# A hybrid decoder layer on one core: the first product of two tiles at a time in seven products of halves

## The chip, the cores and the metric

The kernel runs on one core of a Trainium2 chip. The core has five engines with queues of their own: PE (TensorE, the matrix products; PEld is its loading of weights), DVE (VectorE), ACT (ScalarE), POOL (GpSimd) and SP (SyncE, which here only issues DMAs). Each engine takes its instructions in the order in which they stand, and waits on semaphores for the others. Operands lie in SBUF, products in the eight banks of PSUM, inputs and scratch tensors in DRAM. The metric is the time of one execution on the device, in microseconds; less is better.

## The reference, cut to what matters

One layer of a decoder for 1024 tokens of 1024 channels, float32. The change lies in the first product, z, and in attention's output.

```python
u = rmsnorm(h, mix_pre_norm)
z = u @ w_in                                  # the first product
z_attn, z_rwkv, z_gate = ...                  # 2304, 1696 and 2048 columns
o_attn = dilated_attention_branch(z_attn)     # three groups (dilation 1, 4, 16), four heads each
o_rwkv = rwkv7_time_mix(z_rwkv, ...)
gate_attn, gate_rwkv = split(sigmoid(z_gate), 2)
merged = gate_attn * (o_attn @ w_attn_up) + gate_rwkv * (o_rwkv @ w_rwkv_up)
h = h + rmsnorm(merged @ w_out, mix_post_norm)
...                                           # a dense MLP and a gated input embedding
```

In attention each group gives, for each head, an output and a softmax maximum m and sum den; the heads' outputs are added over the three groups with weights exp(m - M) x den / (their sum).

## The kernel before, in words

**Tiles of the first product.** z is made transposed, in 48 tiles of 128 columns of `w_in` (`wz`): 2 for the low-rank inputs, 12 for the RWKV part, 18 for attention and 16 of gates. u lies transposed in SBUF as `uT[p][h]`: p is the high or the low part of a number (the high part is the value rounded to float32r, the low part the rest), h the half of the tokens. A tile's weights come as `wr` by DMA, ACT copies the high part to `wh`, POOL subtracts it to `wl`. Every product of the kernel is made of three: high x high, high x low, low x high (`mm3`). So a tile is 2 halves of tokens x 8 slices of channels x 3 = 48 matmuls of 128x512, 24 to a PSUM bank. Three banks (`z0`, `z1`, `s0`) rotate. When a bank is full, ACT copies it out: for attention into q, k or v with the tokens reordered by the dilation (`qk`, `v`), for a gate into `gst`, which SP stores in DRAM (`gscr`).

**Attention.** A unit n (0 to 5) is two heads of one group; the groups come in the order 2, 1, 0. A unit has three tiles (q, k, v). q and k are turned by rope: SP swaps their halves into `sw` by DMA, POOL multiplies `sw` by the sines, DVE multiplies by the cosines and adds. v is turned by PE (`av`) and copied to `vkb`. Then come four steps r of two blocks: scores on PE (`sc`), masked maxima on DVE (the rows named ISA in the order, CUSTOM_DVE in the profile, `SB<-sc,amask`), `nm` on DVE (minus the maximum), exponentials on ACT (`SB<-SB,nm`), transposes on PE (`pt`), copies on DVE (`PB`), values on PE (`po`), and ACT copies the output out. The outputs of six units stay in SBUF (`OTA`, `OTB`). After the last step `combine` makes the weights of the sum for all four heads, turns them on PE (`rw`), spreads them with `sel` over the channels (`cb`), and DVE and POOL multiply and add. `oaT` is the result's high and low part.

**The merge.** Eight bodies `merge(j)` multiply the RWKV output (`orT`, tiles `orw`, loaded from DRAM by `load_or`) and `oaT` by `wup`, in `bk` and `z` banks, with two gates read back from DRAM (`g<-gscr`).

**What sets the order.** The program is written by a small planner, `Order`. Attention and RWKV are chains, generators that are resumed at their due time. The tiles are dense work: a list of bodies with a gate (a condition) and a load; whenever no chain is due, the next matmul of the current dense body is issued, and the next body is picked from the list, the first whose gate holds. A gate tile of `wz` can be taken at any time, so it fills what attention leaves open. PE keeps the planner's order to the end. DVE, ACT, POOL and SP keep it up to attention; after that a second scheduler orders their instructions. Tiles in SBUF have tags (`TM0`, `MP`, `px`, ...): a new tile with a tag waits until the old one has been read.

Of the kernel before, what the change touches and what calls it, by code (L numbers as in the profile page):

```python
# [19 lines left out]
T = 1024  # L20
# [115 lines left out]

class Order:
# [41 lines left out]
    def pick(self):  # L179
        for i, (gate, load, body, late) in enumerate(self.dense):  # L180
            if gate() if gate else i == 0:
                del self.dense[i]
                return body(*load()) if load else body(), late
        return None
# [60 lines left out]
def layer(ctx: ExitStack, tc: tile.TileContext, x, pT, wz, wup, w_out, wff1, w_ff2, w_ple, w_pleg,  # L245
# [22 lines left out]
    bv_scr = [dram.tile([128, T], F32, name=f"bvscr{w}") for w in range(NU)]  # L268
    og_scr = [dram.tile([128, T], F32, name=f"ogscr{w}") for w in range(NU)]
# [201 lines left out]
    def add_z(wi, evac, gate=None):  # L471
        def body(hi, lo):
            for h in range(2):
                ps = zbank()
                yield from zhalf(ps, hi, lo, h)
                evac(h, ps)
        sch.add(body, lambda: wload(wz[wi]), gate)

    def add_gate(j):
        def evac(h, ps):  # L480
            st = rtile([128, 512], "gst", "gst")
            S.activation(st, ps, AF.Copy)
            SY.dma_start(g_scr[j][:, h * 512:(h + 1) * 512], st)
        add_z(32 + j, evac, lambda: True)
# [428 lines left out]
    def attn_ok(n, x):  # L913
# [3 lines left out]
        return (("Q", n - 2) if x < 2 else ("vk", n - 1)) in done  # L917

    def add_attn(n):
# [7 lines left out]
        def permuted(dst, ps, h):  # L927
            S.activation(dst.rearrange("p (r i) -> p i r", r=d)[:, h * (L // 2):(h + 1) * (L // 2), :],
                         ps.rearrange("p (i r) -> p i r", r=d), AF.Copy)

        def turned(z, sw):
            G.tensor_tensor(sw, sw, rope_t[g][:, 1], OP.mult)
            V.tensor_tensor(z, z, rope_t[g][:, 0], OP.mult)
            yield max(G.end - sch.t, 0.0) + 1.0
# [3 lines left out]
        def qk(x):  # L938
            def evac(h, ps):
                if h == 0:  # L940
                    A[n][x] = rtile([128, T], "qk", (("r", "Ep"), ("k", "En"))[x][hp])
                    if g not in rope_t:
                        rope_t[g] = rtile([128, 2, T], "rope", f"AR{gi % 2}")
                        SY.dma_start(rope_t[g], rope[g].rearrange("a p t -> p a t"))
                z = A[n][x]
                permuted(z, ps, h)
                if h == 1:
# [4 lines left out]
            return evac  # L952

        def v_evac(h, ps):
            if h == 0:
                A[n]["vx"] = rtile([128, T], "v", "v" if n else "TM0")
            permuted(A[n]["vx"], ps, h)
            if h == 1:
                A[n][2] = A[n]["vx"]
                A[n]["t"] = sch.dep  # L960
        for x, evac in enumerate((qk(0), qk(1), v_evac)):
            add_z(base + x, evac, lambda x=x: attn_ok(n, x))
# [3 lines left out]
    def attention():  # L966
# [33 lines left out]
        def nat(g):  # L1000
            NAT[g] = yield from natural(g, stat)

# [3 lines left out]
        OTA = rtile([128, 2, 2, T], "OTA", "TM0")  # L1006
        OTB = rtile([128, 2, 2, T], "OTB", "TM1")
        OT = {g: (OTA[:, 0], OTA[:, 1], OTB[:, 0])[i] for i, g in enumerate(GORD)}

# [8 lines left out]
        def scores(r):  # L1018
# [29 lines left out]
            if r % 8 == 7:  # L1048
                sch.spawn(nat(g), 2, 5.0)
# [15 lines left out]
        def values(r, po):  # L1065
            n, g, hp = unit(r)
            d = DILS[g]
            vk, out_ = vkb[:, n % 2], OT[g][:, hp]
# [8 lines left out]
            if r % 2:  # L1077
                b = 2 * (r % 4)
                src = po.rearrange("p a b -> p (a b)")
# [9 lines left out]
            if r % 4 == 3:  # L1089
                done.add(("B", n))  # L1090
                if n < 4:
                    sch.spawn(at_last(n + 2), 2)
                else:
                    load_or(5 - n, G)
# [21 lines left out]
        load_or(2, G)  # L1116
        load_or(3, V)
# [700 lines left out]
```

## Time and profile before

| what | us |
|---|---|
| median of 3 runs | 1790.07 (1789.71 to 1792.19) |
| the profiled execution | 1786.45 |
| its span, first to last instruction | 1784.7 |
| PE busy in it | 1751.1 (98%) |
| attention's first scores to its last step | about 523 to 778 |
| last matmul of attention's sum (`cb`) | 804 |
| gate tiles alone | 804 to 832 |
| merge | 832 to 900 |

How the rows are read: a group's row has the engine, the operation, out<-in by the names of tiles, the shape, the count, then the busy time in us and the mean of one in ns, and behind the second bar the idle time just before these instructions with what ended it. A row of the timeline begins with the start and the duration in us. A row of a table of stretches has the length and then each engine's busy time, the granted clock of PE, the share of the DMA engines and GB/s.

### The profile page before, as it was taken

To read this page: it belongs to the slowest core of one execution; us is meant where nothing else is said; L and a number is where in the kernel's file an instruction comes from. 1 tells how busy PE (TensorE), PEld (TensorE's weight loads), DVE (VectorE), ACT (ScalarE), POOL (GpSimd) and SP (SyncE) were. 2 spreads that over 40 slices of the span, in tenths; PEclk is the share of its full clock that TensorE was granted. 3 is DMA by queue.
4 is the path that set the end of the run, shared out by engine and by line. 5 is a ranking of instruction groups with operands and counts; after the bars stand their busy time and mean duration, and the time that the engine had idled before them with its cause. 6 is when DMAs were issued, how large, how long until landed. Compare 5 with 4: busy or idle time off the path is not lost.

```text
span 1784.7 us, 25836 instructions
## 1 busy us (share of the span) xinstructions
PE 1751.1 (98%) x10192; PEld 1430.9 (80%) x10192; DVE 1052.5 (59%) x1866; ACT 728.2 (41%) x1301; POOL 773.6 (43%) x507
## 2 busy tenths in 40 slices
PE   9999989999999999999999999999999999999898
PEld 8787877878877877778888888888888888887786
DVE  6289777766535233353736565655655677888454
ACT  5824433332334343542524533333333333334353
POOL 1344131231232323332230366666666897986411
PEclk9999999999999999999999999999999999999999
DMA  4621121212242222333534211121111111113221
GB/s 161 210 95 37 48 77 42 90 42 95 84 146 77 66 60 71 100 120 133 200 95 142 83 60 59 50 69 48 48 48 48 53 54 48 48 48 100 93 79 48
DMA packets 51546, 146.13 MB, mean 82 GB/s; under 512 B 6241, under 2 KB 6625, under 8 KB 51426
## 3 DMA queue, kind: packets, MB, share of 16 engines
q1 hardware_dynamic: 51426, 144.49, 24.7%
q8 instruction: 80, 1.31, 0.3%
q14 instruction: 40, 0.33, 0.1%
HBM read 110.52 MB, written 27.26 MB: 77 GB/s over the span
## 4 chain that ended last, share of the span: by engine, by line
PE 89%; DVE 5%; ACT 3%; issue 2%; POOL 1%; DMA 0%; DVEq 0%; ACTq 0%; POOLq 0%
PE z L293 19%; PE z L295 19%; PE z L291 19%; PE bk L291 7%; PE bk L295 7%; PE bk L293 7%; DVE tot L116 1%; PE sc L274 1%; PE tp L282 1%; DVE xy L116 1%; PE A L274 1%; PE y L274 1%; PE po L274 1%; PE pt L282 1%; PE wr L274 1%
## 5 line engine op out<-in xcount | busy, mean ns | idle before, releaser
L116 DVE TENSOR_TENSOR tot<-tot,bk 128x512 f32<-128x512 f32 x468 | 308.1, 684 | 188.1 <-PE bk L295 187.4
L116 POOL TENSOR_TENSOR wl<-wr,wh 128x1024 fp32r<-128x1024 f32 (+1 forms) x87 | 211.5, 2431 | 442.2 <-ACT wh L116 423.0
L291 PE MATMUL z<-uh,wh 128*128 128x512 f32 (+1 forms) x800 | 313.6, 392 | 5.8 <-ACT part L116 3.0
L295 PE MATMUL z<-uh,wl 128*128 128x512 f32 (+1 forms) x800 | 314.2, 393 | 2.6 <-POOL wl L116 2.6
L293 PE MATMUL z<-ul,wh 128*128 128x512 f32 (+1 forms) x800 | 315.0, 394 | 0.3 <-DVE ul L116 0.3
L293 PE MATMUL z<-f,wh 128*128 128x512 f32 x496 | 193.1, 389 | 0.2 <-DVE f L116 0.2
L291 PE MATMUL z<-f,wh 128*128 128x512 f32 x496 | 193.2, 389 | 0.1
L295 PE MATMUL z<-f,wl 128*128 128x512 f32 x496 | 193.0, 389 | 0.0
L291 PEld LDWEIGHTS z<-uh,wh 128*128 128x128 f32 x800 | 152.0, 190 | 36.9 <-ACT part L116 3.5
L116 ACT ACTIVATE duo<-sum 128x512 fp32r<-128x512 f32 x150 | 90.3, 625 | 222.2 <-PE bk L295 117.1
L295 PEld LDWEIGHTS z<-uh,wl 128*128 128x128 f32 x800 | 152.0, 190 | 34.2 <-POOL wl L116 4.0
L293 PEld LDWEIGHTS z<-ul,wh 128*128 128x128 f32 x800 | 151.9, 190 | 31.0 <-issue 3.6
L291 PE MATMUL bk<-duo 128*128 128x512 f32 x420 | 163.4, 389 | 0.0
L295 PE MATMUL bk<-duo 128*128 128x512 f32 x420 | 163.4, 389 | 0.0
L293 PE MATMUL bk<-duo 128*128 128x512 f32 x420 | 163.4, 389 | 0.0
L116 POOL TENSOR_TENSOR duo<-sum,duo 128x512 fp32r<-128x512 f32 x75 | 101.1, 1348 | 98.6 <-ACT duo L116 95.8
L116 ACT ACTIVATE wh<-wr 128x1024 fp32r<-128x1024 f32 (+1 forms) x87 | 90.3, 1038 | 115.0 <-PE z L293 82.7
L116 POOL TENSOR_TENSOR sum<-w2r 128x512 f32<-128x512 f32 x75 | 98.8, 1318 | 64.1 <-DMA w2r<-in_w_ff_dram 59.3
L293 PEld LDWEIGHTS z<-f,wh 128*128 128x128 f32 x496 | 93.1, 188 | 19.8 <-DVE f L116 0.5
L291 PEld LDWEIGHTS z<-f,wh 128*128 128x128 f32 x496 | 93.1, 188 | 19.7 <-ACT f L116 0.4
L295 PEld LDWEIGHTS z<-f,wl 128*128 128x128 f32 x496 | 93.1, 188 | 19.3
L116 POOL TENSOR_TENSOR sum<-hr 128x512 f32<-128x512 f32 x75 | 97.6, 1310 | 4.8 <-DVE duo L116 3.1
(310 smaller groups left out, 3217.1 us busy)
## 6 DMA issues: line engine op xcount, KB each, us to landing
wr<-in_wz_dram SPq DMA_DIRECT2D x48, 512.0 KB, 3.9
w2r<-in_w_ff_dram SPq DMA_DIRECT2D x32, 512.0 KB, 3.5
wr<-in_wff_dram SPq DMA_DIRECT2D x31, 512.0 KB, 3.5
xt<-in_x_dram SPq DMA_DIRECT2D x16, 512.0 KB, 4.2
gscr<-gst SPq DMA_DIRECT2D x32, 256.0 KB, 2.1
g<-gscr SPq DMA_DIRECT2D x16, 512.0 KB, 4.2
sw<-qk SPq DMA_DIRECT2D x48, 128.0 KB, 2.3
sascr<-lst SPq DMA_DIRECT2D x16, 256.0 KB, 3.7
```

The lines of the kernel that those rows point to most:

```text
L116: return f(*a, **kw)
L274: PE.matmul(out_, a, b, start=start, stop=stop)
L282: PE.transpose(out_, a, ident if idn is None else idn)
L291: PE.matmul(ps, ah, bh, start=i == 0, stop=False)
L293: PE.matmul(ps, ah, bl, start=False, stop=False)
L295: PE.matmul(ps, al, bh, start=False, stop=i == n - 1)
```

## The change

**Seven products.** The first six tiles of attention and ten gate tiles stay as they were. The other twelve tiles of attention and six gates are taken in nine pairs. For a pair, the weights are four blocks (two tiles by two halves of the 1024 channels, a11 to a22) and u is four (two halves of channels by two halves of tokens). The four results take seven products of a sum of weights with a sum of u's blocks, in place of eight plain ones, 12 matmuls each. The sums of u (`f1`, `f2`, `f3`, `f4`) and their high and low parts (`T[1]` to `T[4]`) are made once, in `seven_operands` and `seven_begin`, from the RWKV part's end to the first pair; `T[1]` is written over a block of `uT`. The sums of weights are made for each pair by DVE (`s1`, `a11`) and POOL (`a21`, `a12`), and each operand is split when one of four buffers (`wh`, `wl`, two each) is free. The first product goes to its place by ACT, every later one is added there by DVE, so a target is finished when its last product is. The pairs are, by number of tile, (6, 7), (8, 11), (9, 10), (12, 13), (14, gate), (15, 16), (17, gate), and two pairs of gates.

**Outputs by way of DRAM.** A unit's output goes to a tile `ot` (tag `MP`, for the last unit `kk`); the first four are stored in `ot_scr` and loaded again, in `back`, when q and k of unit 4 and the last rope are done with.

**The last sum by heads.** `combine` is called twice, for the two heads of hp 0 (after unit 4) and of hp 1 (after unit 5). `load_or` loads the RWKV outputs only after unit 5's last scores. A merge body is picked only when both calls are through and `orT` is complete.

```diff
+    SEVEN = ((1, "a11", (((0, 1), None),)), (2, "a12", (((0, 0), (0, 1)),)), (6, "s2", (((0, 1), (0, 1)),)),
+             (7, "s3", (((1, 0), (0, 1)),)), (5, "s1", (((1, 1), (1, 0)), ((0, 1), (0, 1)))),
+             (3, "s4", (((0, 1), (0, 1)),)), (4, "a22", (((1, 0), (1, 0)),)))
...
+            for i, (n, w, sums) in enumerate(SEVEN):
...
+                seven_split(4, ready)
...
+                ps = zbank()
+                yield from mm3(ps, [(t[:, 0, k * 128:k * 128 + 128], t[:, 1, k * 128:k * 128 + 128]) + b
+                                    for k, b in enumerate(seven_tokens(n))])
...
+                for to, a in sums:
+                    if a is None:
+                        S.activation(at(to), ps, AF.Copy)
+                    else:
+                        V.tensor_tensor(at(to), at(a), ps, OP.add)
...
+        def split(w):
+            if w == "a11":
+                src["s1"] = rtile([128, 512], "s1", "yc")
+                V.tensor_tensor(src["s1"], a21, a22, OP.add)
...
+            if w == "s2":
+                G.tensor_tensor(a21, a11, a21, OP.subtract)
+                V.tensor_tensor(a11, src["s1"], a11, OP.subtract)
+            if w == "s4":
+                G.tensor_tensor(a12, a12, a11, OP.subtract)
+            S.activation(t[:, 0], src[w], AF.Copy)
+            G.tensor_tensor(t[:, 1], src[w], t[:, 0], OP.subtract)
...
-        OTA = rtile([128, 2, 2, T], "OTA", "TM0")
-        OTB = rtile([128, 2, 2, T], "OTB", "TM1")
...
+            yield from wait(lambda: ("Q", 4) in done)
+            t = [rtile([128, T], "ot", x) for x in ("r", "k")]
+            yield from wait(lambda: rot[2] == 4)
+            t2 = rtile([128, 2, T], "ot", "AR0")
...
+                SY.dma_start(OT[GORD[n // 2]][n % 2], ot_scr[n])
...
-        yield from combine(OT, OTB[:, 1], stat, sel)
+            yield from combine(0, OT, tiles, sel)
+            yield from wait(lambda: ("Q", 5) in done)
...
+            yield from combine(1, OT, tiles, sel)
+            done.add("C")
...
+        raw = {w: load(w, x) for w, x in ((0, "a"), (1, "Ep"), (3, "En"))}
+        yield from wait(lambda: ("B", 5) in done and raw[3][1] < sch.t)
+        for w, x, eng in ((0, "UV", G), (1, "BT", V), (3, "BK", G)):
...
+            if w == 0:
+                raw[2] = load(2, "a")
...
-        sch.add(body, load, lambda: ("B", 5) in done)
+        sch.add(body, load, lambda: "C" in done and len(orT) == NU)
```

Three places in the order of the instructions, before and after. First DVE, in the last step of unit 1 (from the copies `PB` of the step before to the next `PB`). Before:

```order
L116 COPY PB<-pt 128x2x128 x2
L116 ISA SB,ast<-sc,amask 128x128
L116 ISA ast 128x1
L116 ISA SB,ast<-sc,amask 128x128
L116 ISA ast 128x1
L116 ISA SB,ast<-sc,amask 128x128
L116 ISA ast 128x1
L116 TENSOR_SCALAR nm<-ast 128x2
```

After:

```order
L116 COPY PB<-pt 128x2x128 x2
L116 TENSOR_TENSOR ul_130<-f_4748,uh_128 128x1024
L116 ISA SB,ast<-sc,amask 128x128
L116 ISA ast 128x1
L116 ISA SB,ast<-sc,amask 128x128
L116 ISA ast 128x1
L116 ISA SB,ast<-sc,amask 128x128
L116 ISA ast 128x1
L116 TENSOR_SCALAR nm<-ast 128x2
```

The low part of `T[1]`, which goes over a block of `uT` (`ul`), now stands ahead of the step's maxima.

Second PE, at attention's end: the last `cb` (the spreading of the sum's weights) and what follows it. Before:

```order
L274 MATMUL cb<-row_6925,sel 128x512 x2
L295 MATMUL z<-uh_123,wl 128x512
L291 MATMUL z<-uh_124,wh 128x512
L293 MATMUL z<-ul_126,wh 128x512
L295 MATMUL z<-uh_124,wl 128x512
```

After:

```order
L282 MATMUL cb<-row_7301,sel 128x512
L299 MATMUL z<-t_4749,wh 128x512
L301 MATMUL z<-t_4750,wh 128x512
L303 MATMUL z<-t_4749,wh 128x512
L282 MATMUL cb<-row_7301,sel 128x512
L299 MATMUL z<-t_4749,wh 128x512
L301 MATMUL z<-t_4750,wh 128x512
L303 MATMUL z<-t_4749,wh 128x512
L299 MATMUL bk<-orw,wh 128x512
L301 MATMUL bk<-orw,wh 128x512
```

Before, 121 matmuls of gate tiles follow the last `cb`; after, three, and then the merge's first product with `orw`.

Third ACT, at the same place, from the copy of the last unit's output to the merge's first gates. Before:

```order
L116 ACTIVATE OTB<-po 128x512
L116 ACTIVATE orw<-wr 128x1024
L116 ACTIVATE wh<-wr 128x1024
L116 ACTIVATE gst<-z 128x512
L116 ACT_TABLE_LOAD
L116 ACTIVATE g<-g 128x1024 x2
L116 ACTIVATE row_6925<-rw 12x512 x2
L116 ACTIVATE gst<-z 128x512
L116 ACTIVATE oah<-OTB 128x512
```

After:

```order
L116 ACTIVATE ast<-ast 128x48
L116 ACTIVATE orw<-orr 128x1024
L116 ACTIVATE row_7301<-rw 12x512 x2
L116 ACTIVATE ot<-po 128x512
L116 ACTIVATE orw<-orr 128x1024 x2
L116 ACTIVATE wh<-wr 128x768
L116 ACTIVATE orw<-orr 128x1024
L116 ACTIVATE wh<-wr 128x768
L116 ACTIVATE oa<-ot 128x512 x2
L116 ACT_TABLE_LOAD
L116 ACTIVATE g<-g 128x1024 x3
```

Before, three of the four `orw` are split ahead of the last output and the first gates' sigmoids ahead of the sum; after, three `orw` come behind the last output, the very last (`orw[2]`) ahead of the result's split (`oa`), and the sigmoids behind that.

381 lines of the change are left out of this document (290 added, 91 removed).

## The prediction

> **What bounds the kernel now.** I read the page first (busy time, then the chain that ended last), then a table of stretches from attention's start to the merge, then the groups of that part by shape, and last the timeline of single steps.
>
> ```profile
> PE 1751.1 (98%) x10192; PEld 1430.9 (80%) x10192; DVE 1052.5 (59%) x1866; ACT 728.2 (41%) x1301; POOL 773.6 (43%) x507
> PE 89%; DVE 5%; ACT 3%; issue 2%; POOL 1%; DMA 0%; DVEq 0%; ACTq 0%; POOLq 0%
> core 0: us, PE busy (x) PEld busy (x) DVE busy (x) ACT busy (x) POOL busy (x), PEclk, DMA share, GB/s
> 576.50:609.00 32.50, 32.50 (x144) 26.85 (x144) 5.13 (x5) 8.64 (x9) 12.93 (x5) 1.00 0.32 89
> 510.00:576.00 66.00, 63.93 (x383) 48.05 (x382) 31.99 (x108) 33.08 (x89) 16.07 (x7) 1.00 0.28 87
> 576.00:746.00 170.00, 170.00 (x954) 134.38 (x953) 54.83 (x164) 66.00 (x147) 55.77 (x21) 1.00 0.25 70
> 746.00:804.00 58.00, 57.90 (x315) 42.37 (x315) 28.96 (x83) 31.23 (x63) 18.51 (x9) 1.00 0.36 123
> 804.00:832.00 28.00, 28.00 (x124) 23.18 (x124) 3.06 (x5) 5.94 (x9) 5.52 (x3) 1.00 0.33 113
> ```
>
> PE carries the chain (89%), and in the stretches that change it never stops: no idle from 576 to 746, 0.1 us up to 804, none to 832. The granted clock (PEclk) is 1.00 throughout. The last stretch is the important one: attention's last sum is done at 804, and PE still has 28 us of gate tiles in hand. That is the slack which hides every late thing of attention. The other engines are a third to a half busy, POOL 55.77 + 18.51 + 5.52 = 79.8 of 256 us, 31%. The row 576.50:609.00 holds 144 matmuls of 512 columns and nothing else: 32.5 / 144 = 0.2257 us each, the price used below.
>
> **The change part by part.** *Removed.* Counted in the order of the instructions, nine pairs of tiles go through seven products of 12 matmuls in place of eight: 9 x 12 = 108 matmuls fewer, 108 x 0.2257 = 24.4 us off a PE that has no idle time there. This is the whole possible gain.
>
> *Added on PE.* The last sum is made for two heads at a time, so its weights are turned twice: 8 transposes more.
>
> ```profile
> L282 PE MATMUL rw<-cs,ast 128*8 128x128 f32 (+1 forms) x24 | 3.1, 272 | 0.0
> L116 POOL TENSOR_TENSOR duo<-sum,duo 128x512 fp32r<-128x512 f32 x75 | 101.1, 1348 | 98.6 <-ACT duo L116 95.8
> L116 POOL TENSOR_TENSOR sum<-w2r 128x512 f32<-128x512 f32 x75 | 98.8, 1318 | 64.1 <-DMA w2r<-in_w_ff_dram 59.3
> L116 ACT ACTIVATE duo<-sum 128x512 fp32r<-128x512 f32 x150 | 90.3, 625 | 222.2 <-PE bk L295 117.1
> L116 POOL TENSOR_TENSOR sw<-sw,rope 128x1024 f32<-128x1024 f32 x11 | 34.7, 3150 | 35.2 <-DMA sw<-qk 32.2 <-PE sc L274 3.0
> L116 DVE TENSOR_TENSOR OTB<-OTB,cb 128x512 f32<-128x512 f32 x4 | 2.7, 678 | 0.0
> L116 DVE COPY row<-rw 8x512 f32<-8x512 f32 x4 | 4.0, 1036 | 0.1
> L116 DVE TENSOR_TENSOR qk<-qk,rope 128x1024 f32<-128x1024 f32 x11 | 13.8, 1253 | 54.8 <-DMA sw<-qk 42.8 <-ACT v L116 11.2 <-ACT SB L116 0.6
> L116 ACT ACTIVATE wh<-wr 128x1024 fp32r<-128x1024 f32 (+1 forms) x25 | 26.0, 1039 | 52.4 <-PE z L293 44.7 <-issue 4.9 <-DMA wr<-in_wz_dram 2.8
> ```
>
> 8 x 3.1 / 24 = +1.0 us, all on the path.
>
> *Seven products' own work.* A pair is 84 x 0.2257 = 19.0 us on PE, a product 2.7 us. Each product's sum leaves PSUM through DVE (a read of SBUF and one of PSUM: 0.68 us; 1.04 where the target is strided). The fifth product has two, at most 2.1 us, and three banks rotate, so I cost this at nothing; if it were bare it would be 0.7 us a product. POOL's share is heavier: seven low parts (1.348) and two sums of weights (1.318) are 12.1 us a pair, and with a unit's two rope multiplications (3.15 each) 18.4 us of 19.0. Where no attention work stretches PE (93 and 116 z matmuls in a row, in pairs 4 and 7, and pair 2) POOL has 0.6 us to spare. Bounds 0 and 6 us (a slip of 2 us in three pairs, since PE has products of four splits ahead); I take 2.0, nearer the lower end since the mean load still fits.
>
> *Operands of the seven products.* Twelve DVE operations of 128x1024 (1.25 each), ten of POOL and eight of ACT (1.04) fall into 510 to 576, where the row shows DVE 32, ACT 33 and POOL 16 of 66 us. The time is free, the places are not: this is the only stretch where PE idles now (66 - 63.93 = 2.1 us). Two places stand in the order. In the last step of unit 1, DVE's low part of uT stands ahead of the masked maxima (ISA rows), and waits for ACT's high part, which waits for PE's last plain tile: 1.04 + 1.25 less the usual lead of 1.2 us (next fence) = 1.1. In step 2 a sum of 1.25 stands ahead of the maxima where the lead is nil. A third, from POOL's low parts blocking DVE, at half an operation, 1.1. Sum 3.5 us, bounds 0 and 8 (every one of the eight steps by 1 us).
>
> *The steps of units 2 to 5.* Sixteen steps go scores, masked maxima (DVE), nm (DVE), exponentials (ACT), transposes (PE), with a fixed number of matmuls between.
>
> ```profile
> 764.17 0.50 ACT L116 ACTIVATE SB<-SB,nm 128x256 f32<-128x256 f32 x1
> 764.57 0.19 ACT L116 ACTIVATION_READ_ACCUMULATOR SB<-SB,nm 128x1 f32 x1
> 765.95 1.09 PE L282 MATMUL pt<-cs,SB 128*128 128x128 f32 x8
> 766.97 1.13 PE L274 MATMUL sc<-qk 64*128 64x256 f32 x8
> L116 DVE TENSOR_SCALAR nm<-ast x48: 154/168/2226, 524.2 to 769.7; 128x2 f32<-128x2 f32 x48
> L116 DVE TENSOR_SCALAR nm<-ast 128x2 f32<-128x2 f32 x48 | 15.0, 332 | 0.3
> 538.40 2.23 DVE L116 TENSOR_SCALAR nm<-ast 128x2 f32<-128x2 f32 x1
> 538.20 2.41 POOL L116 TENSOR_TENSOR wl<-wr,wh 128x1024 fp32r<-128x1024 f32 x1 [8.35 <-PE z L295]
> ```
>
> The exponentials end at 764.76, the transposes start at 765.95: a lead of 1.2 us. The nm operation takes 0.168 us at the median and 2.23 at worst, and the worst one ends at 540.63, as POOL's operation ends (540.61): a nm that meets POOL waits for it. Its mean, 332, is 0.16 us over the median at POOL's 31%. After the change POOL has 63 x 1.348 + 18 x 1.318 + 8 x 3.15 = 134 us more or less fixed in some 235 us, and with the last sum's work 62%: twice the share, so 0.33 us a nm, 0.33 us more a step than now. In the order a DVE eviction (0.68) or an ACT split (0.625) often stands between. All three make 1.6 us against a lead of 1.2: 0.4 us lost in a bad step. With every second step bad, 16 x 0.2 = 3.2 us; bounds 0 and 6.4.
>
> [...]
>
> *DRAM.* Four outputs are stored and read back on SP's queue (512 KB each). The read of units 2 and 3 waits for unit 4's last scores and has pair 7's weights queued behind it; those must wait anyway until pair 6 has given its buffers back, later in the order. Hidden; if not, a weight's landing, 3.9 us (below).
>
> *The end.* The 28 us of spare gate tiles are gone: one to eighteen matmuls stand between the last sum's steps, and the merge follows at once.
>
> ```profile
> 769.83 0.84 DVE L116 TENSOR_TENSOR ast<-ast 128x32 f32<-128x32 f32 x5
> 772.12 0.97 DVE L116 TENSOR_TENSOR ast<-ast 128x32 f32<-128x32 f32 x5 [1.45 <-ACT ast L116]
> 773.51 0.40 DVE L116 TENSOR_TENSOR ast<-ast 128x32 f32<-128x32 f32 x3
> L116 POOL TENSOR_TENSOR orw<-wr,orw 128x1024 fp32r<-128x1024 f32 x3 | 7.5, 2505 | 15.8 <-ACT orw L116 15.8
> L116 ACT ACTIVATE orw<-wr 128x1024 fp32r<-128x1024 f32 x4 | 4.2, 1056 | 3.8 <-issue 2.2 <-DMA wr<-oscr 1.4
> L116 ACT ACTIVATE OTB<-po 128x512 f32<-128x512 f32 x4 | 2.4, 588 | 3.6 <-PE po L274 3.6
> wr<-in_wz_dram SPq DMA_DIRECT2D x48, 512.0 KB, 3.9
> wr<-oscr SPq DMA_DIRECT2D x4, 512.0 KB, 3.2
> g<-gscr SPq DMA_DIRECT2D x16, 512.0 KB, 4.2
> ```
>
> From the last scores' end (766.97 + 1.13 = 768.10) to the weights of the sum (773.91) DVE and ACT need 5.8 us now; with an eviction, two copies of transposes in between and one wait for POOL about 8.5. In the new order PE reaches their transposes after 19 z, the values and a turn: 19 x 0.2257 + 2 x 1.02 = 6.3. A wait of 2.2 us, bounds 0 and 3.5. Then orw[2]: its raw tile is loaded into a tag that another raw tile leaves only after the last values product. Chain: eviction 0.59, ACT 1.06, POOL 2.51, DMA 3.2, ACT 1.06, POOL 2.51 = 10.9 us. PE reaches its second matmul after 1.05 + 39 x 0.2257 = 9.9. That is 1.0, or 3.4 with a landing of 4.2 and POOL at 3.15: I take 2.2.
>
> Sum: -24.4 + 1.0 + 2.0 + 3.5 + 3.2 + 2.2 + 2.2 = -10.3 us. The profiled execution took 1786.45 (span 1784.7); the runs' median is 1790.07, 3.6 more. Against the execution 1776.1, against the median 1779.8.
>
> **The rivals.** *Nothing is lost*: all waits fit into the leads. For it speaks that PE now loses 0.1 us in 228; against, that the 28 us of reserve are gone. -24.4 + 1.0: 1766.7. *Most is lost*: every wait at its upper bound but POOL's slip, -24.4 + 1 + 2 + 8 + 6.4 + 3.5 + 3.4 = -0.1: 1790, no change. *Slower, by POOL*: one mechanism, DVE's nm behind POOL. A collision costs 0.16 / 0.31 = 0.53 us now; if POOL's operations stand back to back, all 48 collide, and if in-order evictions have eaten the lead, nothing covers them: 48 x 0.53 = 25 us on top of the forecast's end terms, -24.4 + 1.0 + 4.4 + 25 = +6: 1796. It decides once a step's delays pass 1.2 us each time. *The change does not do what it says*: fewer than nine pairs. The order shows nine, so next to nothing.
>
> **How the numbers follow.** Forecast (1774 to 1786) 0.47, nothing lost (below 1774) 0.25, most lost 0.14, slower 0.13, the last 0.01. A measurement of this kernel tells 0.2% (3.6 us) from no change. Of the third case a little is still faster: faster 0.74, same 0.13, slower 0.13. The range, 1767 to 1790, runs from nothing lost to no change; the forecast's own is 1774 to 1786.
>
> **What would show it.** PE's waits between 510 and 832: under 3 us means nothing lost. Each step: transposes waiting for SB (ACT) and nm's mean over 0.5 us; rw waiting for ast; bk waiting for orw; z waiting for wl in pairs 2, 4 and 7. The prediction is wrong if the products wait for DVE's evictions, or if a DMA stands in PE's waits for several us.

## The result: 1.1% slower, where 0.6% faster was forecast

The changed kernel takes 1809.76 us (median of 4 runs, 1804.48 to 1812.67), the kernel before 1789.89 beside it: a ratio of 1.0108, 95% interval 1.0081 to 1.0136. The forecast was 1779.8, its range ended at 1790.

The page of the changed kernel, busy time and the chain that ended last:

```profile
PE 1746.5 (96%) x10092; PEld 1418.8 (78%) x10092; DVE 1168.2 (65%) x1982; ACT 731.5 (40%) x1326; POOL 871.1 (48%) x580
PE 74%; DVE 9%; issue 5%; POOL 5%; ACT 4%; DMA 3%; DVEq 0%; SPq 0%; POOLq 0%; ACTq 0%
```

PE has 100 matmuls fewer, 108 less 8 rw (24.4 - 1.0 = 23.4 us), and yet is busy only 4.6 us less; and its share of the chain has fallen from 89 to 74%. So it idles more, and what it does goes slower. Where, the table of stretches tells (length, busy time of PE, PEld, DVE, ACT and POOL, PEclk, DMA share, GB/s): the first eight steps; from there to the first product with `orw`; the merge; the rest. After:

```profile
524.40:591.10 66.70, 56.61 (x321) 41.57 (x321) 49.11 (x116) 34.46 (x89) 34.08 (x16) 0.90 0.20 63
591.10:845.40 254.30, 239.08 (x1288) 181.26 (x1289) 165.84 (x345) 91.89 (x226) 143.54 (x92) 0.99 0.31 93
845.40:917.50 72.10, 66.79 (x278) 53.37 (x277) 50.05 (x65) 34.63 (x42) 16.89 (x9) 0.95 0.60 210
917.50:1810.80 893.30, 876.03 (x3902) 723.31 (x3901) 544.46 (x836) 351.55 (x638) 523.69 (x360) 0.99 0.20 67
```

Before, the same places:

```profile
522.80:575.90 53.10, 52.26 (x322) 38.70 (x321) 28.20 (x102) 26.20 (x79) 13.15 (x6) 1.00 0.26 79
575.90:831.35 255.45, 255.35 (x1388) 199.46 (x1389) 86.84 (x251) 102.61 (x217) 79.90 (x33) 1.00 0.29 87
831.35:894.25 62.90, 62.90 (x278) 51.89 (x277) 44.10 (x60) 30.33 (x39) 13.31 (x7) 1.00 0.54 186
894.25:1784.70 890.45, 873.69 (x3902) 722.32 (x3901) 547.13 (x835) 348.63 (x635) 522.26 (x359) 0.99 0.20 66
```

The same 321 matmuls of the first eight steps take 13.6 us more. The long stretch has 100 matmuls fewer and is only 1.2 us shorter. The merge's same 278 matmuls take 9.2 us more, the rest 2.9, the start 1.6: 13.6 - 1.2 + 9.2 + 2.9 + 1.6 = 26.1, the difference of the two spans. PEclk has left 1.00 in the first three.

The 2.9 us of the rest are not the change's. Some 750 and 770 us behind the merge PEclk falls to one half in both kernels. In this execution of the kernel before it did so for 3.4 us each time (0.51 from 1640.7 to 1644.1, 1.00 from there to 1647.5), in that of the changed kernel for twice as long (0.50 from 1663.9 to 1667.3 and on to 1670.7). The part behind the merge took 893.2 us also in before_less, told of below, whose end is that of the kernel before.

PE's longest waits from 510 to 920 (in total, times, longest):

```profile
PE pt L290 <- ACT SB L116: 12.0, 9, 5.4
PE rw L290 <- DVE ast L116: 6.2, 2, 3.4
PE bk L299 <- ACT wh L116: 3.5, 1, 3.5
```

The longest one, on the timeline (DVE, POOL and PE; start, duration):

```profile
543.04 3.37 DVE L116 TENSOR_TENSOR qk<-qk,sw 128x1024 f32<-128x1024 f32 x1 [4.47 <-POOL sw L116]
546.33 2.30 DVE L116 TENSOR_SCALAR nm<-ast 128x2 f32<-128x2 f32 x1
...
540.63 2.38 POOL L116 TENSOR_TENSOR sw<-sw,rope 128x1024 f32<-128x1024 f32 x1
542.97 2.35 POOL L116 TENSOR_TENSOR t<-f,t 128x1024 fp32r<-128x1024 f32 x1
545.29 3.32 POOL L116 TENSOR_TENSOR t<-f,t 128x1024 fp32r<-128x1024 f32 x1
...
549.21 0.86 PE L290 MATMUL pt<-cs,SB 128*128 128x128 f32 x2 [5.35 <-ACT SB L116]
```

Two things add up here. First DVE's queue stands 4.47 us, since the last sum of rope waits for POOL's product with the sines (`sw`), and that stands in POOL's queue behind two low parts of u's sums (`t`, 5.75 us from 534.91). Then POOL makes two more low parts in a row. The sum of rope (1.22 alone) lasts 3.37 beside the first: it ends at 546.41, 1.1 us, about its own length, behind POOL's 545.32. Then nm, of two numbers a partition, lasts 2.30 and ends with the second. The exponentials wait for nm, PE for them, 5.35 us.

The second kind of stop is unit 3's last step:

```profile
712.22 0.69 DVE L116 TENSOR_TENSOR s<-wr 128x512 f32<-128x512 f32 x1 [1.40 <-DMA wr<-in_wz_dram]
714.35 1.76 DVE L116 TENSOR_TENSOR wr<-s,wr 128x512 f32<-128x512 f32 x1 [1.44 <-POOL wr L116]
717.23 1.01 DVE L116 COPY PB<-pt 128x256 f32<-128x256 f32 x2
...
713.05 1.27 POOL L116 TENSOR_TENSOR wr<-wr 128x512 f32<-128x512 f32 x1 [2.92 <-DVE s L116]
...
718.85 1.44 PE L290 MATMUL rw<-cs,ast 128*8 128x128 f32 x6 [2.86 <-DVE ast L116]
```

The sums of the next pair's weights stand on DVE ahead of the copies and maxima. The first waits for its weights' DMA, the second for POOL, which still reads the same tile, and is held by POOL's next operation. That is 3.9 us for two operations of 0.69, with the step's copies and maxima queued behind.

And a third thing, that no term of the prediction had. PEclk in the 4 us behind the stop at 549:

```profile
550.00:554.00 4.00, 4.00 (x16) 0.50 0.00 0
```

PE runs at half speed there, though it is busy all the time.

### The profile page after: what moved, and what is told of

The parts are those of the page before. It is cut to its first block, busy times and chain, and to the rows that moved or that the text cites. A ratio compares the mean times of both kernels' runs of the same rounds, so it can differ in the third digit from the quotient of the medians.

```text
span 1810.8 us, 25984 instructions
## 1 busy us (share of the span) xinstructions
PE 1746.5 (96%) x10092; PEld 1418.8 (78%) x10092; DVE 1168.2 (65%) x1982; ACT 731.5 (40%) x1326; POOL 871.1 (48%) x580
## 4 chain that ended last, share of the span: by engine, by line
PE 74%; DVE 9%; issue 5%; POOL 5%; ACT 4%; DMA 3%; DVEq 0%; SPq 0%; POOLq 0%; ACTq 0%
PE z L303 15%; PE z L301 15%; PE z L299 15%; PE bk L299 6%; PE bk L303 6%; PE bk L301 6%; DVE tot L116 2%; DMA g<-gscr 1%; POOL wl L116 1%; PE tp L290 1%; DVE xy L116 1%; PE A L282 1%; PE fq L282 1%; PE y L282 1%; PE wr L282 1%
## 5 line engine op out<-in xcount | busy, mean ns | idle before, releaser
L116 POOL TENSOR_TENSOR wl<-wr,wh 128x1024 fp32r<-128x1024 f32 (+1 forms) x69 | 168.5, 2442 | 283.7 <-ACT wh L116 269.4
L299 PE MATMUL z<-uh,wh 128*128 128x512 f32 (+1 forms) x584 | 231.1, 396 | 6.8 <-ACT part L116 3.0
L303 PE MATMUL z<-uh,wl 128*128 128x512 f32 (+1 forms) x584 | 231.4, 396 | 2.7 <-POOL wl L116 2.7
L301 PE MATMUL z<-ul,wh 128*128 128x512 f32 (+1 forms) x584 | 231.6, 397 | 0.3 <-DVE ul L116 0.3
L299 PEld LDWEIGHTS z<-uh,wh 128*128 128x128 f32 x584 | 112.8, 193 | 29.6 <-ACT part L116 3.6
L116 ACT ACTIVATE wh<-wr 128x1024 fp32r<-128x1024 f32 (+2 forms) x96 | 88.2, 919 | 117.5 <-PE z L301 37.4
L303 PEld LDWEIGHTS z<-uh,wl 128*128 128x128 f32 x584 | 112.6, 193 | 25.1 <-POOL wl L116 4.0
L301 PEld LDWEIGHTS z<-ul,wh 128*128 128x128 f32 x584 | 113.0, 193 | 21.5 <-issue 1.4
```

The lines of the kernel that those rows point to most:

```text
L116: return f(*a, **kw)
L299: PE.matmul(ps, ah, bh, start=i == 0, stop=False)
L301: PE.matmul(ps, ah, bl, start=False, stop=False)
L303: PE.matmul(ps, al, bh, start=False, stop=i == n - 1)
```

## The experiments

Ratios are to the kernel before, run beside; the changed kernel's is 1.0108. 0.1% is 1.8 us.

**no_sums.** The sums of u and their splits left out:

```diff
-        T[4] = rtile([128, 4, 512], "t4", "AR1", F32R), rtile([128, 4, 512], "t4", "BK2", F32R)
...
+        T[4], T[2] = U(0, 1), U(1, 1)
```

> The changed kernel without the sums of u: T[1] to T[4] are plain blocks of u, so nothing is added and nothing is split for them (the results of the seven products are then not z). PE's order stays the same. Theory P (the sums' work on POOL, and what it holds up on DVE, makes the stops in attention's first eight steps): from the first scores to the eighth step's values PE needs about 54 us as before the change, in place of 66.7, its idle time there falls from 11 to under 3 us, and the whole is 11 to 15 us under the changed kernel, about 1796. Rival Q (the steps are late by their own new order, not by the sums): the stretch stays above 63 us and the whole within 4 us of the changed kernel.

1796.34 us, 1.0045 (1.0028 to 1.0063): 13 us less by the medians, 11 by the ratios, and the first steps take 54.0 us. Theory P holds: the sums cost 11 to 13, not the forecast 3.5.

**sums_dve.** POOL's ten operations for these sums on DVE:

```diff
+                            e.eng = nc.vector
                             e.tensor_tensor(p(o), p(ins[0]), p(ins[1]), ins[2])
+                            e.eng = nc.gpsimd if e is G else nc.vector
```

> The changed kernel with the ten POOL operations of the sums of u (128x1024, 2.4 to 2.9 us each) given to DVE (1.2 us each), all else and PE's order as it was. Theory P (a DVE operation that meets a POOL operation waits until it ends): nm and the last sum of rope in the first eight steps take 0.17 and 1.25 us again, in place of up to 2.3 and 3.4, and of the 13.6 us that the stretch has lost 7 to 11 come back, about 1800. Rival Q (it is the queue of DVE that is too long; ten operations more make it longer by 12 us in 67): the same or slower than the changed kernel, 1808 to 1818.

1799.43, 1.0056 (1.0041 to 1.0071): 9 to 10 of these come back, though DVE has ten operations more. So the length of DVE's queue is not the cost; what POOL does to it is. That is two things, and this run takes both away at once: the hold, and DVE's wait for POOL's `sw` (4.5 us in these steps in the changed kernel, none here). The changed kernel's stops of PE at 533 and 536 (1.30 and 1.59 us) came with no such wait, but with nm at 1.71 and 2.07; how the 9 to 10 us divide between the two was not measured. PE's wait for SB in these steps falls from 9.9 to 2.2 us.

**nm_act.** nm on ACT:

```diff
+        class OnAct:
+            @staticmethod
+            def tensor_scalar(out_, in_, a, b, op0):
+                return nc.scalar.activation(out_, in_, AF.Copy, scale=a)
...
+                V.eng = OnAct
                 V.tensor_scalar(nm, mx, -SCALE, None, op0=OP.mult)
+                V.eng = nc.vector
```

> The changed kernel with nm made on ACT (a copy with a scale) in place of DVE's tensor_scalar, in all 24 steps; PE's order stays. Theory P says that 20 of 48 nm met POOL and took 0.92 us in place of 0.17, and that this stands on the path of a step: PE's wait for SB falls from 12.0 us to 4 to 8 and the whole by 4 to 8 us, 1802 to 1806; the one case of 3.4 us in the sum of rope stays. Rival R (nm's waits lie in the lead that a step has, and the rest of DVE's queue decides): within 2 us of the changed kernel.

1808.56, 1.0102 (1.0085 to 1.0119): nothing, as rival R says. PE's wait for SB falls from 12.0 to 6.6 us, and that for PB grows from 1.7 to 6.4. The timeline tells why (DVE, then POOL, then PE):

```profile
545.86 3.40 DVE L116 TENSOR_TENSOR qk<-qk,sw 128x1024 f32<-128x1024 f32 x1 [6.06 <-POOL sw L116]
549.30 3.25 DVE L116 TENSOR_TENSOR f<-f,uh 128x1024 f32<-128x1024 f32 x1
...
548.14 3.32 POOL L116 TENSOR_TENSOR wl<-wr,wh 128x1024 fp32r<-128x1024 f32 x1
...
552.93 0.91 PE L282 MATMUL po<-PB,vkb 128*64 128x128 f32 x6 [4.75 <-DVE PB L116]
```

With nm gone, DVE still waits 6.06 us for POOL's `sw`, the operations of two inputs in SBUF are held in nm's place, and the copies `PB` stand behind them. It is DVE's queue that POOL stops, not one operation in it.

**ladder.** The kernel before, with ever more delay in sixteen steps:

```diff
+                if r >= 8 and b % 2 == 0:
+                    for _ in range(4 + 3 * (r - 8)):
+                        nc.vector.tensor_scalar(nm, nm, 1.0, None, op0=OP.mult)
```

> The kernel before the change, with a delay in the sixteen steps of units 2 to 5: 4, 7, 10 ... 49 extra DVE operations on nm of 0.12 to 0.16 us each, so the exponentials come 0.5 to 7 us later and PE stops for 0 to 5 us, longer from step to step. Theory C (after a stop of PE of 2.9 us or more, PE runs at half clock for some us): stops up to 1.7 us are followed by matmuls of 512 columns at 0.226 us, stops from 2.9 us by 3 to 12 such matmuls at 0.427, a loss of 0.8 to 2.6 us each time, with a granted clock of 0.6 to 0.7 there. Rival H (the low clock after the stops of the changed kernel comes from the heavier work of the other engines or from the DMAs): no slow matmuls in the stretch whatever the stop. In both the time is about 1790 + 33 us; by C some 5 to 10 us more.

1882.88 us, 93 over the kernel before: more delay than the 33 us meant. The author put that down to small operations that met POOL, which was not counted. The stops reach 10.6 us. The clock behind the stops of 1.1, 3.9, 8.1 and 10.6 us:

```profile
671.00:676.00 5.00, 5.00 (x29) 1.00 0.00 0
681.00:686.00 5.00, 5.00 (x18) 0.50 0.28 101
758.00:762.00 4.00, 4.00 (x18) 0.53 0.02 4
813.00:817.00 4.00, 4.00 (x17) 0.58 0.00 0
```

The order of PE is that of the kernel before, so each matmul's lateness can be followed from stop to stop. Two stops of 0.9 and 1.1 us cost 0.3 us beyond themselves. Eleven of 2.4 to 10.6 us cost 1.7 to 3.1 more, 2.3 on the mean. The spans differ by 96.4 us (1881.1 and 1784.7), of which these thirteen stops themselves are 66.9. Theory C holds but for its sizes (a loss of 2.6 us at most, stops from 2.9 us on), and the heavier load of the other engines is not needed for it: here it is that of the kernel before. The changed kernel has five such places more than before (537, 550, 720, 831, 877; at 537 two stops of 1.3 and 1.6 us came within 3 us), so by an estimate of 5 x 2.3 some 11 of the 49 us (26.1 + 23.4) that its profiled execution lost.

**wsums_dve, no_wsums, wsums_out.** From here on the edits are on top of sums_dve (1799.43), but for eight (on the changed kernel) and before_less (on the kernel before). First the sums of weights: POOL's two on DVE; left out; left out with PE's order kept.

```diff
+            G.eng = nc.vector
             if w == "s2":
                 G.tensor_tensor(a21, a11, a21, OP.subtract)
...
             if w == "s4":
                 G.tensor_tensor(a12, a12, a11, OP.subtract)
+            G.eng = nc.gpsimd
```

This is wsums_dve; in no_wsums and wsums_out none of the four is made.

> The kernel with the sums of u on DVE (1799.4), and besides all four sums of weights of a pair on DVE (two were on POOL, and DVE's second waits for POOL's first, which reads the same tile); PE's order stays. Theory P (DVE waits for POOL and is held by it, with the masked maxima of the next step behind): the wait of rw at 714 (2.8 us) goes, and PE idles 3 to 6 us less from 592 to 845 (now 13), 1793 to 1797. Rival Q (DVE's queue is too long as it is, 64% busy, and 18 more operations of 0.69 us lengthen it): the same or up to 5 us slower.

> The kernel with the sums of u on DVE (1799.4), with the sums of weights left out (the seven operands are plain blocks of the weights, so the results are not z). It bounds what the sums of weights cost on DVE and POOL. Theory P: PE's idle time from 592 to 845 falls from 13 to under 7 us and the whole by 5 to 9, 1790 to 1794. Rival Q (the additions by which DVE empties the banks, 0.68 to 1.1 us each, delay the steps): idle stays above 10 us, the whole within 3 us.

> The kernel with the sums of u on DVE (1799.4), with the sums of weights left out as in no_wsums (results are not z), but this time with PE's order kept exactly as in that kernel; no_wsums had its own order, in which PE's waits for maxima and copies fell from 8.1 to 2.5 us and those for rope's result rose from 2.6 to 9.4. Theory P (DVE's and POOL's work for the weights makes the steps of units 2 to 5 late): PE's waits for SB, PB and ast from 581 to 832 fall from 8.1 to under 3 us, those for rope stay near 2.6, the whole 4 to 8 us under 1799.4. Rival Q: they stay above 6 us, the whole within 3 us of 1799.4.

wsums_dve: 1800.56, 1.0076 (1.0053 to 1.0099), no gain; the wait for POOL is gone, but eighteen operations more stand ahead of copies and maxima, and rw still waits 2.6 us. no_wsums: 1793.77, 1.0035 (1.0020 to 1.0050); the planner had another order there, in which three scores wait 9.4 us for rope. wsums_out, in the same order: 1785.10, 0.9991 (0.9978 to 1.0004). So the sums of weights cost 14 us by the medians, 12 by the ratios, as much as the sums of u. Why they cost as much in wsums_dve, where DVE waits for POOL no more, its timeline shows at unit 3's last step:

```profile
701.26 1.58 DVE L116 TENSOR_TENSOR wr<-wr 128x512 f32<-128x512 f32 x1
```

This sum meets a low part on POOL (701.01 to 702.30) and is held; with the other three it takes 3.6 us ahead of that step's maxima (0.69 + 1.58 + 0.68 + 0.68), where the two operations and their wait took 3.9.

**s_late.** The same number of sums, elsewhere: s3 = a11 - a21 is made as a22 - s2, after DVE is through.

```diff
-            if w == "a11":
-                src["s1"] = rtile([128, 512], "s1", "yc")
-                V.tensor_tensor(src["s1"], a21, a22, OP.add)
...
             if w == "s2":
-                G.tensor_tensor(a21, a11, a21, OP.subtract)
+                src["s1"] = rtile([128, 512], "s1", "yc")
+                V.tensor_tensor(src["s1"], a21, a22, OP.add)
                 V.tensor_tensor(a11, src["s1"], a11, OP.subtract)
+            if w == "s3":
+                G.tensor_tensor(a21, a22, a11, OP.subtract)
```

> The kernel with the sums of u on DVE (1799.4), with the same number of sums of weights at other places: DVE's first sum is issued two operands later, when its weights have long landed, and POOL's difference is taken from DVE's result, so that DVE waits neither for a DMA nor for POOL there; before it waited 6.3 us for the DMA of wr and 6.5 for POOL's wr from 592 to 845. PE's order is nearly the same. Theory D (what the sums of weights cost, 11.6 us in all, is the waiting of DVE in them with copies and maxima queued behind): 6 to 10 us less, 1789 to 1793, PE's wait of 2.8 us for ast goes. Rival L (it is their length and POOL's hold): within 3 us of 1799.4.

1784.08, 0.9962 (0.9949 to 0.9976): 15 us less by the medians, 17 by the ratios, as much as leaving the sums out or a little more, and more than theory D's 6 to 10. It is the fastest of the kernels that compute the whole layer, 0.4% faster than the kernel before. PE's order is not quite the same, but it does not explain this: PE reaches both rw that waited in sums_dve (2.8 and 1.4 us) two and five matmuls earlier, and waits for neither. DVE's waits in sums_dve from 581 to 832:

```profile
DVE wr L116 <- POOL wr L116: 6.5, 6, 1.5
DVE s L116 <- DMA wr<-in_wz_dram: 6.3, 4, 1.8
```

and what is left of them in s_late (a wait of 0.6 us for POOL's wh besides, 2.1 in sums_dve):

```profile
DVE s L116 <- DMA wr<-in_wz_dram: 6.5, 4, 2.1
```

The second sum's durations (min/median/max, ns) in sums_dve:

```profile
L116 DVE TENSOR_TENSOR wr<-s,wr x8: 691/1016/1767, 597.5 to 790.1; 128x512 f32<-128x512 f32 x8
```

and in s_late:

```profile
L116 DVE TENSOR_TENSOR wr<-s,wr x8: 676/692/693, 594.4 to 778.4; 128x512 f32<-128x512 f32 x8
```

Unit 3's last step on s_late's timeline:

```profile
696.18 0.69 DVE L116 TENSOR_TENSOR s<-wr 128x512 f32<-128x512 f32 x1 [1.24 <-DMA wr<-in_wz_dram]
696.96 0.69 DVE L116 TENSOR_TENSOR wr<-s,wr 128x512 f32<-128x512 f32 x1
```

The wait for the DMA is still there, against what the edit was to do; what went is the wait for POOL and the hold behind it. Two operations take 1.5 us in place of 3.9, and from 580 to the merge PE waits 0.2 us each for SB and PB and not at all for ast. So theory D holds by its half on POOL, the waiting and the hold together; its size was forecast too small.

**eight.** The changed kernel's frame with eight plain products a pair:

```diff
-                    else:
-                        V.tensor_tensor(at(to), at(a), ps, OP.add)
...
+                        if k:
+                            S.activation(at((m, h)), ps[h].rearrange("p (i r) -> p i r", r=d), AF.Copy)
```

> The changed kernel with eight plain products a pair in place of seven: no sums of u or of weights, 24 matmuls to a bank, ACT copies it out; 108 matmuls more. Pairs of tiles, outputs by way of DRAM, the sum by heads and the late load of the RWKV outputs stay, and 102 matmuls stand again between the last cb and the merge. Theory E (these other parts cost little; what was lost is the work that used to cover the steps and the merge's loads, and the new work on DVE and POOL): 1787 to 1794, as before the change, PE idle under 5 us from 592 to the merge and no wait above 2 us in the merge. Rival O (outputs by way of DRAM, the sum by heads and the late load cost by themselves): above 1797, with rw, po or orw among PE's waits.

1795.42, 1.0042 (1.0020 to 1.0063). The stretches, as above:

```profile
522.50:575.30 52.80, 51.96 (x321) 38.72 (x321) 27.35 (x102) 26.41 (x81) 13.69 (x7) 1.00 0.29 89
575.30:833.80 258.50, 257.28 (x1397) 200.30 (x1398) 95.47 (x269) 101.42 (x233) 80.89 (x50) 1.00 0.33 102
833.80:897.60 63.80, 63.29 (x278) 51.84 (x277) 43.73 (x60) 29.57 (x37) 13.81 (x7) 1.00 0.54 184
```

Between the theories: outputs by way of DRAM, the sum by heads and the late load cost 3.1 us in the long stretch (1.5 for rw among them) and 0.9 in the merge, with 102 matmuls in hand; no wait is over 1.2 us. The spans differ by 6.4 us, 3.0 of it behind the merge, where before_less, with the end of the kernel before, is longer by 2.7 as well: not the change's. By the ratio these parts cost 4 to 11 us of the 19: a part of what made the kernel slow, not the larger one.

**before_less.** That the merge lost 9 us for want of work in hand was the next idea. The kernel before, two gate tiles fewer:

```diff
-    for j in range(16):
+    for j in range(14):
         add_gate(j)
```

> The kernel before the change with two of the sixteen gate tiles left out (the merge takes two other gates in their place, so the result is not the reference's): 96 matmuls fewer, and PE's order is the same but for the matmuls between the last cb and the merge, 25 in place of 121. 96 x 0.2257 = 21.7 us of PE's work is gone, nothing else is added or moved. Theory E (this work covered the merge's loads and sigmoids): the merge then loses 5 to 10 us to stops and half clock, and the whole gains only 12 to 17 us, 1771 to 1776. Rival W (the work is worth what it takes): 20 to 22 us faster, about 1767, merge at 62.9 us from its first product to its last as before.

1767.86, 0.9869 (0.9849 to 0.9890): 21 us faster by the medians, 20 to 27 by the ratio, for 21.7 us of work. Theory E falls. This is for work at the end; what matmuls are worth that are taken out of attention it does not show. The merge takes 65.1 us with 25 matmuls ahead of it, 2.2 more than before:

```profile
573.40:807.20 233.80, 233.65 (x1295) 181.50 (x1294) 86.53 (x251) 98.29 (x211) 75.16 (x31) 1.00 0.29 86
807.20:872.30 65.10, 63.51 (x278) 51.71 (x277) 42.61 (x59) 29.94 (x38) 13.67 (x7) 1.00 0.54 180
```

**wo_late, wo_spread, g_early.** What is late in the merge, then? Of the changed kernel, SP's loads and PE:

```profile
853.48 0.38 SPq L133 DMA_DIRECT2D wr<-in_w_out_dram  x1
860.64 0.38 SPq L133 DMA_DIRECT2D wr<-in_w_out_dram  x1
862.33 6.27 SPq L133 DMA_DIRECT2D wr<-in_w_out_dram  x2
871.16 0.34 SPq L133 DMA_DIRECT2D wr<-in_wup_dram  x1
...
875.05 0.51 PE L299 MATMUL bk<-orw,wh 128*128 128x512 f32 x1 [3.45 <-ACT wh L116]
```

The fourth body's weights (`in_wup`) stand behind four loads of the next product's. wo_late moves these to the sixth body, wo_spread to one each in the third to sixth, g_early (on top of s_late) loads the first two bodies' gates early as well:

```diff
-            if j == 1:
+            if j == 5:
                 wo[0] = wo_half(0, GA)
```

> The kernel with the sums of u on DVE (1799.4), and besides the first half of w_out loaded from the sixth merge body on in place of the second (its four DMAs stand ahead of the third and fourth body's weights on SP's queue). Theory M (the stop of 3.5 to 4.3 us in the merge is these weights' landing, behind w_out's loads): PE's wait for wh in the merge goes, and the half clock of 2.5 us behind it, so 4 to 7 us less, 1792 to 1795. Rival N (the weights are late since the gates' buffers are not free, so w_out's place does not matter): within 1.5 us of 1799.4.

> The kernel with the sums of u on DVE (1799.4), with the four loads of w_out's first half one each in the third to sixth merge body (now all four in the second). Theory M: with room on SP's queue and on DVE between them, no weights of the merge are late, the stop of 4.3 us goes without the one of 2.7 us that came when all four stood in the sixth body, and the merge takes 64 to 66 us in place of 72: 5 to 9 us less, 1790 to 1794. Rival N (the merge begins without any work in hand, so that one of its operands is late wherever w_out stands): 1796 or more.

> The kernel with the later sums of weights (s_late, 1784.1), with the gates of the first two merge bodies loaded ahead of the last sum into TM0 and TM1, which are free by then (they were loaded into a, px and AR0, which the last sum and the RWKV outputs hold to the end), and w_out's first half from the sixth body on. Theory B (the merge loses 8 us since the tags of its gates come free late, not since there is no work in hand): the merge's excess over the kernel before falls from 8.3 to under 4 us, the whole is 3 to 6 us faster, 1778 to 1781. Rival N (another operand is late in their place: weights of wup, RWKV outputs, DVE's products): the excess stays above 6 us and the whole within 2 us of 1784.

wo_late: 1794.09, 1.0041 (1.0028 to 1.0055), a median in theory M's range, but by the ratios an interval that overlaps with that of sums_dve; the stop of 4.3 us is gone, and at 885.76 bk waits 2.7 us for DVE. wo_spread: 1793.80, 1.0042 (1.0026 to 1.0058), the same, with 4.2 us of waits for DVE; its merge does not come down to the 64 to 66 us of theory M. g_early: 1787.17, 0.9994 (0.9983 to 1.0006), by the ratios 0.3% slower than s_late, so theory B falls. In it the later bodies run without a stop up to 870, but the first waits for the RWKV outputs:

```profile
818.42 0.74 PE L299 MATMUL bk<-orw,wh 128*128 128x512 f32 x1 [2.37 <-ACT orw L116]
822.23 0.79 PE L301 MATMUL bk<-orw,wh 128*128 128x512 f32 x1 [3.07 <-POOL orw L116]
822.82 0.63 PE L303 MATMUL bk<-orw,wl 128*128 128x512 f32 x1
823.25 0.63 PE L299 MATMUL bk<-orw,wh 128*128 128x512 f32 x1
823.67 0.63 PE L301 MATMUL bk<-orw,wh 128*128 128x512 f32 x1
```

Weights, gates and RWKV outputs are all loaded at the end only; one made early, the next is late, and the merge stays 7 to 11 us longer than before the change. Which of the change's end terms makes it so was not settled: `eight` has the same gate of the merge and the same tags with 102 matmuls ahead of it, and lost 0.9. Not tried: a third pair of tiles for the gates.

**rw_late, three, four.** The two rw elsewhere; that with wo_spread and nm on ACT; s_late with wo_spread and rw_late:

```diff
-                sch.spawn(nat(g), 2, 5.0)
+                sch.spawn(nat(g), 2, 3.0)
...
-        yield None
+        yield sch.until(sch.dep + 3.5)
```

> The kernel with the sums of u on DVE (1799.4), with the two rw that PE waits for at another place: the transposes of unit 3's maxima behind 13 matmuls after that unit's last scores (they stood behind the next unit's first scores), and those of the last sum 14 matmuls behind the last transposes in place of 2. Theory: PE's wait for ast falls from 4.2 us to under 1.5 and the half clock behind the stop of 2.8 us goes, 3 to 6 us less, 1793 to 1796. Rival (the chain of the last sum only waits later, at cb or in the merge, since the matmuls put ahead are missing behind): within 2 us of 1799.4.

> All four together: sums of u on DVE, w_out's loads spread over four merge bodies, the two rw moved, and nm made on ACT. If the parts are independent, 1799.4 less 6 (w_out) less 4 (rw) less 1 to 3 (nm, now that DVE's other operations of the first steps no longer meet POOL): 1785 to 1790, as the kernel before the change or a little faster. If the lost time only moves from wait to wait (no work in hand at the end): 1793 or more.

> Sums of u on DVE, sums of weights at the later places, w_out's loads spread over four merge bodies, the two rw moved. If the four are independent and theory D holds: 1799.4 - 8 - 2.5 - 2.5 = 1786, about the kernel before the change. If time only moves on to the merge, which has no work in hand: 1791 or more.

rw_late: 1794.06, 1.0042 (1.0023 to 1.0061), as its theory said by the median, by the ratios no clear gain on sums_dve; rw waits for ast no more, two scores wait 1.9 us for DVE's `row` in its place. three: 1796.02, 1.0065 (1.0040 to 1.0091), no better than its parts, if not worse; what nm on ACT does there was not followed. four: 1785.81, 0.9979 (0.9966 to 0.9992), no better than s_late alone: with DVE's waiting gone, rw had nothing left to give, and the merge kept its 8 us. That this time is the 1786 of the first theory is luck: one of the four parts gave all of it, and more than it was put at.

## Why the prediction was wrong

*What PE's work is worth*: right, as far as before_less shows it: 20 to 27 us for 96 matmuls put at 21.7.

*The products' own work*: right within its bounds. No product waits over 0.3 us for an eviction, and z waits 0.7 us for wl, where 2.0 was forecast.

*Operands of the seven products, 3.5 us with bounds 0 and 8*: the first step that failed. Measured 11 to 13. The rows for it were quoted (nm at 2.23 us beside POOL), but a collision was priced at half an operation, 1.1 us, once, and the rows were of nm alone. POOL's operations came two in a row, the two-input sums of DVE were held up to 3.4 us as well as nm, and the step's whole queue stood behind them. That POOL's own queue would make `sw` late, and DVE wait 4.5 us for it, was in no term. In the changed kernel `qk<-qk,sw`, with two inputs in SBUF, took 3.37 for 1.22 beside POOL, while an eviction with one input in PSUM (`gst<-gst,z`) took 0.67 beside POOL's `wr` at 716.04, and none of the 18 from 510 to 930 over 0.69.

*The steps of units 2 to 5, 3.2 us with bounds 0 and 6.4*: the second step that failed, and the larger. Measured 12 to 17 for the sums of weights alone. The bound came from nm, an eviction and a split; the sums of weights stood in the sum as load on POOL and as nothing on DVE. That one of them waits for POOL, with copies and maxima of the step behind it in DVE's queue, was not asked, though the same question was put for SP's queue. The nm that the term did price was not the cost: in the long stretch it takes 0.32 us on the mean in the changed kernel, 0.49 in s_late, which is far faster.

*The end, 2.2 and 2.2*: rw's stop was 3.35 in the profiled execution, within its bounds of 0 and 3.5. `orw` made PE wait 0.4. The merge's 9.2 us were in no term: 5.3 us of stops (72.10 - 66.79), 3.5 of them for the fourth body's weights, and 3.9 more of busy time (66.79 for 62.90) with the half clock in it. What made these loads late stays open.

*DRAM*: hidden, as forecast; PE's waits from 510 to 920 name no outputs read back, neither in the changed kernel nor in eight.

*A stop's price*: missing altogether. Every term counted the idle time only. Five stops bring 2.3 us each on top, by ladder.

*The rival "slower, by POOL"*, 1796 and 13%, had the mechanism. Its place was wrong: nm in units 2 to 5, where it came from the sums of u in units 0 and 1 and from sums of weights. nm_act shows that nm was not even necessary for it.

Added up from the runs, as an estimate: the saving of 24.4; the sums of u 11 to 13 and the sums of weights 12 to 17, with the half clock that they bring; the other parts 4 to 11 by eight; the merge 8 more than in eight. That is 11 to 25 us slower, and 19 were measured. The two terms that failed were put at 3.5 and 3.2 and cost 23 to 30.

What s_late leaves against the 24.4 us: it gains 15 in the long stretch, and gives back 3.5 in the first eight steps, 8.5 in the merge and 2.7 behind it (as in before_less). That leaves this execution, at 1786.33, even with the kernel before; the median of s_late's runs is 1784.08:

```profile
522.87:579.50 56.63, 53.82 (x321) 39.87 (x320) 44.75 (x120) 34.58 (x89) 16.30 (x9) 0.97 0.24 74
579.50:820.00 240.50, 235.92 (x1290) 179.27 (x1289) 163.57 (x345) 92.28 (x227) 141.81 (x92) 1.00 0.32 99
820.00:891.40 71.40, 66.79 (x279) 53.75 (x279) 49.99 (x67) 36.52 (x44) 17.28 (x9) 0.95 0.61 210
```

## What to carry to other kernels

When work is added to an engine that is half idle, ask not whether it has the time but what each new instruction waits for and what stands behind it in that engine's queue: four sums a pair cost 12 to 17 us while they waited for another engine or were held by it, and nothing that could be measured when they were not. In ladder a stop of PE of 2.4 to 10.6 us cost its length plus 2.3 us on the mean, and in the changed kernel two of 1.3 and 1.6 us close together brought the half clock too. And before a saving is counted, leave the work out of the old kernel and time that: before_less took one run and told that the work was worth what it was put at, so that the loss had to lie in what was added or moved.

## What the runs showed of the hardware

Half clock sets in sooner than expected. In the changed kernel, from 510 to 930, each of the four stops of PE of 2.86 us or more is followed by it (2.86, 3.35, 3.45 and 5.35 us, with PEclk at 0.50 behind them); of shorter ones two close together are (1.30 and 1.59 us, ending at 533.26 and 535.56), while a single one of 1.56 us, ending at 661.16, is not. In the kernel before no stop there is over 1.2 us, and PEclk stays at 1.00. In the run three a single stop of 1.49 us ends at 649.21, and PEclk is 0.50 from 650.4 to 653.7; in sums_dve one of 1.56 us at the same place ends at 651.24, and PEclk is 1.00 from 651.3 to 656. The shortest of the eleven in ladder had 2.45 us (at 740). So these runs give no sharp bound between 1.5 and 2.4 us. At half clock matmuls of 512 columns come every 0.43 us (rows at 822.82 to 823.67 of g_early), up to twelve of them in a row (877.53 to 882.23 in the changed kernel), then every 0.2257 again. The half clock lasted 3.4 us (537.5 to 540.9 in the changed kernel), or two or three times that (875.5 to 882.3, 544.3 to 554.5), and could begin within the stop (at 718.4, where the stop ends at 718.85). What makes the loss vary from 1.7 to 3.1 us was not shown.

The hold between DVE and POOL goes both ways in the changed kernel: POOL's 128x1024 takes 2.35 to 2.4 us alone and up to 3.4 beside a two-input sum of DVE (`t<-f,t` 2.35 to 3.43), and that sum 1.2 alone and up to 3.4 (`qk<-qk,sw` 1.21 to 3.37).
